# An encoder layer with a seven-product MLP: another order of the up blocks and of the preparation of their inputs, and all weight sums finished in device memory ahead of the MLP

## The chip, the cores and the metric

The kernel runs on one core of one Trainium2 chip. The metric is the device time of one execution in microseconds; a time below is the median of several executions, and the profile shows a single one of them.

## The reference, cut to what matters

One encoder layer (512 tokens, width 1024) and a final norm, all in float32: a token mixer of two kinds of recurrent heads with one input and one output projection, a cross attention over 256 memory tokens, and an MLP of width 4096.

```python
x = x + token_mixer(rmsnorm(x, norm_mix), w_in, b_in, ..., w_out)
x = x + cross_attention(rmsnorm(x, norm_xattn), rmsnorm(mem, norm_mem), w_q, w_kv, w_o)
x = x + squared_relu_mlp(rmsnorm(x, norm_mlp), w_up, w_down)
return rmsnorm(x, norm_final)

def squared_relu_mlp(xn, w_up, w_down):
    return jnp.square(jax.nn.relu(xn @ w_up)) @ w_down
```

## The kernel before

**Products.** Each float32 operand is split in two parts by `split_out` (the line L325): a copy on ACT (ScalarE) gives the high part, a subtraction on DVE (VectorE) the low one, and a product is three matmuls on PE (TensorE): high by high, high by low, low by high. The weights' parts are the tiles `wh` and `wl`. They are held in pools of three buffers, so that the split of a block's weights can begin only when the block three places ahead of it is through on PE. The weights are loaded into tiles `st`, also three buffers, by DMA on SP's queue (L245 before the MLP; L282, L1215 in it).

**The MLP.** It is cut into four quarters, each an up stage (even numbers, 0 to 6) and a down stage (odd, 1 to 7). Every stage is a 2 by 2 block product done with seven products P1 to P7 in place of eight, and each product has two groups a and b, so that a stage has 14 blocks. A block of an up stage is 24 matmuls of 256 columns (the loop over L1559, L1560, L1561), a block of a down stage 12 of 512 columns (L1283, L1284, L1285). The seven products need sums of weights and sums of inputs. The inputs' sums and their splits are the **forms**: for the first up stage they are made in `norm_half` from the normed residual (`times_r` multiplies by the norm's factor, then `part_split` or `split_out`); for a down stage they are made from the squared up results by `first` (L1527, a P5 input), `second` (L1531, P6), `by_p7` (L1539) and `by_p3` (L1535), each an operation on DVE followed by a split. The split's tiles are named `a4` in the program's order and `a` in the profile; `xT` and `yT` are the up stages' inputs, `vv` the residual, `rg` the norm's factor row among others.

**PE's order** is the order in which the code is written; for the MLP that is the table `MORDER`, a string such as "1a 2a 1b" per up stage. DVE, ACT, POOL (GpSimd) and SP each run in the order that a scheduler found from priorities (`tc.high_priority()` moves an operation to the front) and from explicit pairs, `behind(a, b)`. Each engine takes its instructions strictly in that order, so one that waits holds up all behind it. Up results lie in PSUM banks; P1, P5 and P6 are copied out of them on ACT (P5's copy is L1575, P6's L1579), and a product that accumulates in the same bank (P3 on that of P5) waits for the copy.

**The sums of weights.** Some of the weight sums are added by POOL's accumulating DMAs into SBUF tiles `as` while the kernel runs. The others are written once to device memory, as `form_...`, and loaded by L1215 when they are needed. `make_forms` has 80 steps for them: each sum is a copy on SP's queue (L282 from the weights, or L298 from another sum, for a second sum that builds on a first) and an accumulating DMA on POOL (L282). A step is taken on each call of `weights()` from the seventh on, and what is then left over at one step per block of the odd MLP stages, in `mahead`:

```python
        if i >= 6:
            next_form()
        return hl_tiles[i]
```

**Ahead of the MLP** stands the attention's output product; its columns are added to the residual in `add_out` (L1371), the sum of squares goes through POOL (L1420), and small matmuls (L1397, L1438 and their like) turn the row of norm factors into the layout of the inputs. `last_made`, `q_made` and `x_made` hold the instructions of a split, for `behind`.

Of the kernel before, what the change touches and what calls it, by code (L numbers as in the profile page):

```python
# [14 lines left out]
ALU = mybir.AluOpType  # L15
# [65 lines left out]
def trunk(ctx: ExitStack, tc: tile.TileContext, x, mem, wpk, vec, cst, lmask, rmask, rows, out):  # L81
# [177 lines left out]
    def weights(key):  # L259
        i = SIDX[key]  # L260
        with (tc.high_priority() if i > 2 else ExitStack()):
            for n in range(i, i + 3):
                split(n)
            load(i + 3)
        if i >= 6:
            next_form()
        return hl_tiles[i]

# [55 lines left out]
    def split_out(dst_hi, dst_lo, src):  # L324
        return sc.activation(dst_hi, src, AF.Copy), v.tensor_tensor(out=dst_lo, in0=src, in1=dst_hi.bitcast(F32), op=ALU.subtract)  # L325
# [167 lines left out]
    for t, ps in enumerate(acc_v):  # L493
        part_v(t, 3)
        d = VV()
# [700 lines left out]
    seq = lambda s: [("P" + w[0], "ab".index(w[1])) for w in s.split()]  # L1196
    MORDER = []
    for q in range(4):
        MORDER += [seq("1a 2a 1b 6a 5a 7a 3a 4a 5b 6b 2b 7b 3b 4b" if q else "1a 2a 1b 2b 5a 5b 3a 6a 6b 7a 7b 4a 3b 4b"),
                   two(*("P1", "P5", "P6", "P2", "P7", "P3", "P4") if q < 3 else ("P1", "P5", "P2", "P6", "P3", "P7", "P4"))]  # L1200
    MJ = [(st, p, g) for st in range(8) for p, g in MORDER[st]]
    mst, mhl, msum = {}, {}, []
# [29 lines left out]
    def msplit(n):  # L1232
        if n >= len(MJ):
            return
        if n not in mhl:
            for w in [w for w in due if w[0] <= n]:
                due.remove(w)
                w[1](*w[2:])
            st, p, g = MJ[n]
            mload(n)  # L1240
            hi, lo = T("wh", 1024, 3, F32R), T("wl", 1024, 3, F32R)
            last_made[0] = split_out(hi, lo, mst[n])[1]
            mhl[n] = (hi, lo)
            if st % 2 and p == "P6":
                due.append((n + 1, sum_add, st, "P4", g))
            if st % 2 and p in ("P5", "P4") and st < 7:
                q = {"P5": "P5", "P4": "P6"}[p]
                due.append((n + 3, sum_base, st + 2, q, g))
                due.append((n + 7, sum_add, st + 2, q, g))
        return mhl[n]  # L1250
# [117 lines left out]

    def add_out(t, c, ps, sign, last):
        z = xr[t, c]  # L1370
        v.tensor_tensor(out=z, in0=z, in1=ps, op=ALU.add if sign > 0 else ALU.subtract)  # L1371
        if not last:
            return
        with (tc.high_priority() if (t, c) in ((1, 1), (3, 0)) else ExitStack()):
            stats(st2, t, c)
            if (t, c) in ((1, 1), (3, 0)):
                rstd_half(t // 2)
        if (t, c) == (2, 0):
            turn_x2[0] = [smb(), smb()]
            later.append([1, lambda: flip(turn_x2[0], (2,), 0)])  # L1380
        elif (t, c) == (3, 0):
            later.append([0, lambda: flip(turn_x2[0], (3,), 0)])
            later.append([1, lambda: norm_half(1)])
        elif t % 2:
            later.append([0 if (t, c) == (1, 1) else 3, lambda: flip([smb(), smb()], (t - 1, t), c)])
            if (t, c) == (1, 1):
                later.append([1, lambda: norm_half(0)])
# [24 lines left out]
    def rstd_half(u):  # L1412
# [6 lines left out]
        rt[u] = tiny(2)  # L1419
        pool_add[0] = gp.tensor_tensor(out=rt[u], in0=m2_, in1=nh.to_broadcast([P, 2]), op=ALU.pow)  # L1420

    def times_r(x, u, h):
        z = x[:, h * 512:h * 512 + 512]
        r = rrow[:, u * 256:u * 256 + 256]
        v.tensor_tensor(out=z.rearrange("p (k t) -> p k t", t=256), in0=z.rearrange("p (k t) -> p k t", t=256),
                        in1=r.unsqueeze(1).to_broadcast([P, 2, 256]), op=ALU.mult)

    def part_split(p, x, h):
        z = slice(h * 512, h * 512 + 512)
        split_out(xf[p][0][:, z], xf[p][1][:, z], x[:, z])  # L1430

    def norm_half(u):

        ps = smb()
        for t in range(2):
            pe.transpose(ps[:, t * P:t * P + P], rt[u][:, t:t + 1].to_broadcast([P, P]), ident)
        with tc.high_priority():
            sc.activation(rrow[:, u * 256:u * 256 + 256], ps[:, 0:256], AF.Copy)  # L1438
            for p, x in ((("P1", fx[0, 0]), ("P2", fx[0, 1])) if u == 0 else (("P5", sraw[0]),)):
                for h in range(2):  # L1440
                    times_r(x, u, h)
                    part_split(p, x, h)
        if u == 0:
            return
        d = sraw[0]
        x1, x3_, x2_, x4 = fx[0, 0], fx[0, 1], fx[1, 0], fx[1, 1]
        v.tensor_tensor(out=d, in0=d, in1=x1, op=ALU.subtract)
        v.tensor_tensor(out=x3_, in0=x3_, in1=d, op=ALU.add)
        split_out(*xf["P3"], x3_)
        split_out(*xf["P6"], d)  # L1450
        for h in range(2):
            times_r(x2_, 1, h)
        v.tensor_tensor(out=x1, in0=x1, in1=x2_, op=ALU.subtract)
        split_out(*xf["P7"], x1)
        for h in range(2):
            times_r(x4, 1, h)
        split_out(*xf["P4"], x4)

    for p in range(4):
        sta_o[p]["P1"] = tuple(t[:, 0:256] for t in os_[p])  # L1460
# [5 lines left out]
        xf[p] = [YT1()[:, :], YT1()[:, :]]  # L1466
    rrow = RG()
    by_blocks(-1, sta_o, (mm2, mm2, sm2, sm2), add_out, heads_in, after_product)
    msum.append(A16())
    due.extend((2 + g, sum_add, 1, "P5", g) for g in range(2))  # L1470
    due.extend((3 + 2 * g, sum_base, 1, "P6", g) for g in range(2))
# [40 lines left out]
    def up(st):  # L1512
# [8 lines left out]
        def form(p, g, src, buf):  # L1521
            t = buf(F32R)
            split_out(t[:, 0:512], t[:, 512:1024], src)
            forms[p, g] = t

        def first(g):
            v.tensor_tensor(out=y[3, g], in0=y[2, g], in1=y[3, g], op=ALU.subtract)  # L1527
            form("P5", g, y[3, g], A4)
# [11 lines left out]
            form("P7", g, y[0, g], A4)  # L1540

        yt = lambda dt: YT1(dt)
        for n, (p, g) in enumerate(MORDER[st]):
            hi, lo = mahead(len(JOBS) * st + n)
            if p == "P1":
                A[g] = smb()
            if p == "P2":
                B[g] = mmb()
            if p == "P5":
                C[g] = mmb()  # L1550
            ps = B[g] if p == "P2" else C[g] if p in ("P5", "P3") else A[g]
            xh, xl = xf[p]
            for k in range(2):
                o = ps[:, k * 256:k * 256 + 256]
                for kt in range(4):
                    z = slice(k * 512 + kt * P, k * 512 + kt * P + P)
                    m = slice(kt * 256, kt * 256 + 256)
                    new = k == kt == 0 and p in ("P1", "P2", "P5")
                    pe.matmul(o, lhsT=hi[:, z], rhs=xh[:, m], start=new, stop=False, **fl)  # L1559
                    pe.matmul(o, lhsT=hi[:, z], rhs=xl[:, m], start=False, stop=False, **fl)  # L1560
                    pe.matmul(o, lhsT=lo[:, z], rhs=xh[:, m], start=False, stop=kt == 3, **fl)  # L1561
                after_product()
            if p == "P1":
                y[0, g] = msum[g][:, 2048:2560]
                with tc.high_priority():
                    sc.activation(y[0, g], ps, AF.Copy)
            elif p == "P2":
                with tc.high_priority():
                    v.tensor_tensor(out=y[0, g], in0=y[0, g], in1=ps, op=ALU.add)
                square(y[0, g], y[0, g])  # L1570
                form("P1", g, y[0, g], yt)
            elif p == "P5":
                y[3, g] = T2()[:, 0:512]
                with tc.high_priority():
                    sc.activation(y[3, g], ps, AF.Copy)  # L1575
            elif p == "P6":
                y[1, g] = rrow[:, (1 - g) * 512:(1 - g) * 512 + 512]
                with tc.high_priority():
                    sc.activation(y[1, g], ps, AF.Copy)  # L1579
            if p in ("P3", "P6") and {("P3", g), ("P6", g)} <= set(MORDER[st][:n + 1]):  # L1580
                z = y[1, g]
                v.tensor_tensor(out=z, in0=C[g], in1=z, op=ALU.subtract)
                square(z, z)
                form("P2", g, z, G4)
            if p == "P7":
                with tc.high_priority():
                    v.tensor_tensor(out=y[3, g], in0=y[3, g], in1=ps, op=ALU.subtract)
                square(y[3, g], y[3, g])
                form("P4", g, y[3, g], A4)
            elif p == "P4":  # L1590
                y[2, g] = T2()[:, 0:512]
                square(y[2, g], ps)
                first(g)
                if g == 0:
                    second(g)
                    by_p7(g)
                    by_p3(g)
        sta = [{} for _ in range(4)]

        def hand(g):  # L1600
# [114 lines left out]
```

## Time and profile before

| What | Value |
| --- | --- |
| Median of three runs (lowest, highest) | 850.69 us (849.35, 851.29) |
| Profiled execution | 848.46 us |
| Its span | 846.6 us |
| PE, busy | 812.1 us, 96% |
| DVE, ACT, POOL, busy | 620.3, 488.1, 92.4 us |
| DMA moved | 165.16 MB, of it 39.85 MB by POOL's queue |
| MLP's first and last matmul | 492.97 us, 838.04 us |

The profiled execution stands 2.2 us below the median; 1.9 us of it lie outside the span. All times inside the profile count from the span's start. "PE mm L1559 <- ACT t L1575" reads: the matmul of line 1559 into a tile mm waited for ACT's instruction of line 1575, which writes t. A row "690.10:693.50 3.40, 1.66 (x14)" of the table by stretches gives a stretch, its length, and the busy time and number of instructions of each engine in it, then PE's granted clock as a share of full speed and the DMA engines' busy share.

### The profile page before, as it was taken

The page shows a single profiled execution, that of the slowest core. Times are in us where ns is not written, and L with a number is a line of the kernel's source. Part 1 is how long each engine was busy: PE and PEld are TensorE (multiplying, and loading weights), DVE is VectorE, ACT ScalarE, POOL GpSimd, SP SyncE. Part 2 cuts the span into 40 slices and gives each one's busy share as a digit, 9 for nine tenths or more (in the row PEclk, how much of TensorE's full clock was granted, in tenths as well). Part 3 has the DMA queues.
Part 4 walks back from the last instruction along what each step waited for, and adds up shares of the span by engine and source line. Part 5 has one row for each costly group of instructions (what it writes and reads, how often), then busy time and mean ns, then how long its engine had stood idle before and what let it go on. Part 6 is the DMA issues. An engine that isn't in the chain of part 4 may idle for free.

```text
span 846.6 us, 14075 instructions
## 1 busy us (share of the span) xinstructions
PE 812.1 (96%) x5438; PEld 699.7 (83%) x5438; DVE 620.3 (73%) x1033; ACT 488.1 (58%) x854; POOL 92.4 (11%) x132
## 2 busy tenths in 40 slices
PE   8999999999999999999999989989998999999995
PEld 6788788877889988888888879868996799889984
DVE  6568875898479897545669889886487658875885
ACT  5247464536586575445455677833683458446854
POOL 2002000220111201202200011020102000100001
PEclk9999999999999999999999999989999999999998
DMA  7367744494478697877635559589998785768462
GB/s 270 115 232 185 218 146 138 100 223 136 165 176 210 187 301 245 229 220 175 173 102 130 120 134 299 164 213 313 298 304 187 212 263 175 199 202 236 160 149 100
DMA packets 56021, 165.16 MB, mean 195 GB/s; under 512 B 5329, under 2 KB 5457, under 8 KB 55954
## 3 DMA queue, kind: packets, MB, share of 16 engines
q1 hardware_dynamic: 40624, 123.94, 42.1%
q0 software_dynamic: 15040, 39.85, 26.0%
q8 instruction: 43, 0.70, 0.3%
q10 hardware_dynamic: 290, 0.47, 0.2%
q14 instruction: 24, 0.20, 0.1%
HBM read 162.14 MB, written 44.04 MB: 244 GB/s over the span
## 4 chain that ended last, share of the span: by engine, by line
PE 61%; DMA 12%; DVE 11%; issue 7%; ACT 6%; POOL 1%; POOLq 0%; ACTq 0%; SPq 0%; DVEq 0%
PE mm L328 10%; PE mm L330 10%; PE mm L329 9%; DMA st<-form_P 5%; DVE wl L325 5%; PE sm L1283 4%; PE sm L1284 4%; PE sm L1285 4%; DMA st<-in_wpk 4%; ACT wh L325 3%; PE mm L1559 1%; PE mm L1560 1%; PE mm L1561 1%; PE sm L1559 1%; PE sm L1561 1%
## 5 line engine op out<-in xcount | busy, mean ns | idle before, releaser
L325 DVE TENSOR_TENSOR wl<-st,wh 128x1024 fp32r<-128x1024 f32 x163 | 199.0, 1222 | 116.6 <-ACT wh L325 115.2
L325 ACT ACTIVATE wh<-st 128x1024 fp32r<-128x1024 f32 x163 | 172.1, 1058 | 186.5 <-PE mm L329 44.0
L328 PE MATMUL mm<-xT,wh 128*128 128x512 f32 x288 | 115.5, 402 | 0.0
L330 PE MATMUL mm<-xT,wl 128*128 128x512 f32 x288 | 113.2, 393 | 0.1
L329 PE MATMUL mm<-xT,wh 128*128 128x512 f32 x288 | 112.7, 391 | 0.3 <-DVE xT L1042 0.3
L1283 PE MATMUL sm<-wh,a 128*128 128x512 f32 x180 | 71.8, 399 | 7.9 <-ACT a L325 5.9
L1284 PE MATMUL sm<-wl,a 128*128 128x512 f32 x180 | 71.5, 397 | 2.3 <-DVE wl L325 2.3
L1285 PE MATMUL sm<-wh,a 128*128 128x512 f32 x180 | 71.3, 396 | 0.5 <-DVE a L325 0.5
L330 PEld LDWEIGHTS mm<-xT,wl 128*128 128x128 f32 x288 | 54.1, 188 | 11.7 <-DVE wl L325 0.3
L329 PEld LDWEIGHTS mm<-xT,wh 128*128 128x128 f32 x288 | 54.2, 188 | 10.9 <-DVE xT L1042 0.9
L328 PEld LDWEIGHTS mm<-xT,wh 128*128 128x128 f32 x288 | 54.1, 188 | 10.8 <-ACT wh L325 0.3
L282 POOL DMA_DIRECT2D as<-in_wpk x24 | 22.0, 957 | 246.9 <-DVE wl L325 138.8
L282 POOL DMA_DIRECT2D form_P<-in_wpk x40 | 43.4, 1459 | 49.4 <-DMA form_P<-form_P 47.4
L1283 PEld LDWEIGHTS sm<-wh,a 128*128 128x128 f32 x180 | 34.5, 192 | 16.4 <-ACT a L325 6.3
L1284 PEld LDWEIGHTS sm<-wl,a 128*128 128x128 f32 x180 | 34.6, 192 | 10.4 <-DVE wl L325 3.2
L1285 PEld LDWEIGHTS sm<-wh,a 128*128 128x128 f32 x180 | 34.4, 191 | 8.3 <-DVE a L325 1.1
L1560 PE MATMUL sm<-xT,wh 128*128 128x256 f32 x128 | 37.1, 290 | 1.3 <-DVE xT L325 1.2
L1559 PE MATMUL sm<-xT,wh 128*128 128x256 f32 x128 | 37.4, 292 | 0.4 <-ACT xT L325 0.4
L1561 PE MATMUL sm<-xT,wl 128*128 128x256 f32 x128 | 36.9, 288 | 0.0
L325 ACT ACTIVATE wh<-as 128x1024 fp32r<-128x1024 f32 x26 | 27.2, 1054 | 16.7 <-PE sm L1285 9.4
L1559 PE MATMUL sm<-yT,wh 128*128 128x256 f32 x128 | 36.3, 284 | 0.4 <-ACT rg L1579 0.4
L1559 PE MATMUL mm<-xT,wh 128*128 128x256 f32 x128 | 36.6, 286 | 0.0
(388 smaller groups left out, 2129.3 us busy)
## 6 DMA issues: line engine op xcount, KB each, us to landing
st<-in_wpk SPq DMA_DIRECT2D x123, 512.0 KB, 4.6
form_P<-in_wpk POOLq DMA_DIRECT2D x40, 512.0 KB, 10.0
st<-form_P SPq DMA_DIRECT2D x40, 512.0 KB, 5.9
as<-in_wpk POOLq DMA_DIRECT2D x28, 512.0 KB, 8.3
form_P<-in_wpk SPq DMA_DIRECT2D x24, 512.0 KB, 6.7
form_P<-form_P SPq DMA_DIRECT2D x16, 512.0 KB, 6.6
gate<-in_wpk POOLq DMA_DIRECT2D x8, 512.0 KB, 5.5
as<-in_wpk SPq DMA_DIRECT2D x8, 512.0 KB, 4.2
```

Of the source, the lines that this page charges most:

```text
L282: return eng.dma_start(out=dst, in_=mblock(st, g, *b), max_dma_last_dim=4096, **kw)
L325: return sc.activation(dst_hi, src, AF.Copy), v.tensor_tensor(out=dst_lo, in0=src, in1=dst_hi.bitcast(F32), op=ALU.subtract)
L328: pe.matmul(ps, lhsT=ah, rhs=bh, start=first, stop=False)
L329: pe.matmul(ps, lhsT=ah, rhs=bl, start=False, stop=False)
L330: pe.matmul(ps, lhsT=al, rhs=bh, start=False, stop=last)
L1283: pe.matmul(ps, lhsT=ah, rhs=bh, start=new, stop=False, **fl)
L1284: pe.matmul(ps, lhsT=ah, rhs=bl, start=False, stop=False, **fl)
L1285: pe.matmul(ps, lhsT=al, rhs=bh, start=False, stop=end and k == 1, **fl)
L1559: pe.matmul(o, lhsT=hi[:, z], rhs=xh[:, m], start=new, stop=False, **fl)
L1560: pe.matmul(o, lhsT=hi[:, z], rhs=xl[:, m], start=False, stop=False, **fl)
L1561: pe.matmul(o, lhsT=lo[:, z], rhs=xh[:, m], start=False, stop=kt == 3, **fl)
```

## The change

1. `weights()` takes a second step of `make_forms` whenever its number divides by four, so that the steps come to an end ahead of the MLP.
2. `MORDER` has other strings for the up stages. The down stages' strings are as before.
3. In `add_out` the additions for (2,0) and (3,0) get high priority. In `norm_half`, P2's first `times_r` comes behind the second split of P1, and the sum for P3 and its split are moved to the end; the split of the MLP's second block of weights comes behind P1's second split.
4. In the up stages `first` gets high priority, and `by_p3(0)` is called once both of its inputs are there, P4a's result and the P2 form of group a (which needs P3a and P6a): with the new strings that is at P4a in three of the four stages, and at P3a in the first.

The lines behind each edit shift: L1371 becomes L1375, L1425 L1431, L1527 L1539, L1531 L1543, L1535 L1547, L1539 L1551, L1559 to L1561 become L1572 to L1574, L1575 L1588, L1582 L1595, L1283 to L1285 become L1286 to L1288, L1490 L1502.

```diff
-        if i >= 6:
+        for _ in range((i >= 6) + (i >= 6 and i % 4 == 0)):
             next_form()
...
-        MORDER += [seq("1a 2a 1b 6a 5a 7a 3a 4a 5b 6b 2b 7b 3b 4b" if q else "1a 2a 1b 2b 5a 5b 3a 6a 6b 7a 7b 4a 3b 4b"),
+        MORDER += [seq("1a 5a 1b 6a 2a 3a 7a 5b 6b 4a 2b 7b 3b 4b" if q else "1a 1b 2a 2b 5a 5b 6a 6b 7a 7b 4a 3a 4b 3b"),
...
-            last_made[0] = split_out(hi, lo, mst[n])[1]
+            made = split_out(hi, lo, mst[n])
+            last_made[0] = made[1]
+            if n == 1:
+                q_made[0] = made
...
-        v.tensor_tensor(out=z, in0=z, in1=ps, op=ALU.add if sign > 0 else ALU.subtract)
+        with (tc.high_priority() if (t, c) in ((2, 0), (3, 0)) else ExitStack()):
+            v.tensor_tensor(out=z, in0=z, in1=ps, op=ALU.add if sign > 0 else ALU.subtract)
...
-                    times_r(x, u, h)
-                    part_split(p, x, h)
+                    t_ = times_r(x, u, h)
+                    if p == "P2" and h == 0:
+                        behind(t_, x_made[0][1])
+                    made = part_split(p, x, h)
+                    if p == "P1" and h == 1:
+                        x_made[0] = made
...
         v.tensor_tensor(out=d, in0=d, in1=x1, op=ALU.subtract)
-        v.tensor_tensor(out=x3_, in0=x3_, in1=d, op=ALU.add)
-        split_out(*xf["P3"], x3_)
         split_out(*xf["P6"], d)
...
         split_out(*xf["P4"], x4)
+        v.tensor_tensor(out=x3_, in0=x3_, in1=d, op=ALU.add)
+        split_out(*xf["P3"], x3_)
...
+    for a, b in zip(q_made[0], x_made[0]):
+        behind(a, b)
...
+                done.add(("P2", g))
+                if ("P4", 0) in done and g == 0:
+                    by_p3(0)
...
-                first(g)
+                with tc.high_priority():
+                    first(g)
+                done.add(("P4", g))
                 if g == 0:
                     second(g)
                     by_p7(g)
-                    by_p3(g)
+                    if ("P2", 0) in done:
+                        by_p3(g)
```

Where the written order and the scheduler move instructions shows in the rows of each engine's order. `a4_`, `xT_`, `t2_` and the like are tiles with their number, `wl<-st,wh` is a weight split.

First place, DVE in stage 1 (the first down stage), before: `t2_823` is the tile that `first` and `second` of group b rework, `a4_854` the low part of P5b's input, `a4_863` that of P6b's; `wl_867` and `wl_870` are the weights of P6a and P6b.

```order
L325 TENSOR_TENSOR wl_867_5691<-as_792_5111,wh_866_5690 128x1024
L325 TENSOR_TENSOR a4_846_5567<-as_739_4829,a4_846_5567 128x512
L325 TENSOR_TENSOR a4_847_5571<-rg_700_4641,a4_847_5571 128x512
L325 TENSOR_TENSOR wl_870_5711<-as_792_5111,wh_869_5710 128x1024
L1527 TENSOR_TENSOR t2_823_5356<-t2_853_5636,t2_823_5356 128x512
L325 TENSOR_TENSOR a4_854_5640<-t2_823_5356,a4_854_5640 128x512
L1531 TENSOR_TENSOR t2_823_5356<-t2_823_5356,as_792_5111 128x512
```

The same place after; P5b's input is now `a4_851`, made from the L1539 row.

```order
L1539 TENSOR_TENSOR t2_823_5372<-t2_850_5618,t2_823_5372 128x512
L325 TENSOR_TENSOR a4_843_5549<-as_739_4845,a4_843_5549 128x512
L325 TENSOR_TENSOR wl_858_5662<-as_739_4845,wh_857_5661 128x1024
L1547 TENSOR_TENSOR rg_700_4657<-rg_700_4657,t2_818_5338 128x512
L1595 TENSOR_TENSOR rg_700_4657<-mm_822_5347,rg_700_4657 128x512
L1502 TENSOR_TENSOR vv_528_3640<-vv_528_3640,sm_855_5659 128x512
L325 TENSOR_TENSOR wl_861_5680<-as_739_4845,wh_860_5679 128x1024
L1502 TENSOR_TENSOR vv_529_3642<-vv_529_3642,sm_856_5660 128x512
L325 TENSOR_TENSOR a4_851_5622<-t2_823_5372,a4_851_5622 128x512
```

`first` of group b and the split of P5b's input moved from behind the weights of P6a and P6b to ahead of both.

A little later on DVE, after: the rows of `second` of group b (L1543) and of P6b's input `a4_863`; `wl_874` and `wl_877` are the weights of P2a and P2b.

```order
L325 TENSOR_TENSOR wl_874_5753<-st_859_5665,wh_873_5752 128x1024
L1543 TENSOR_TENSOR t2_823_5372<-t2_823_5372,as_792_5127 128x512
L1551 TENSOR_TENSOR as_792_5127<-as_792_5127,t2_850_5618 128x512
L1547 TENSOR_TENSOR rg_700_4657<-rg_700_4657,t2_823_5372 128x512
L325 TENSOR_TENSOR wl_877_5771<-st_862_5683,wh_876_5770 128x1024
L325 TENSOR_TENSOR a4_863_5701<-t2_823_5372,a4_863_5701 128x512
```

`second` stood one row behind the split of P5b's input before; now seven rows, three of them weight splits, lie between, and P6b's split stands behind P2b's weights.

Second place, DVE at the start of the first up stage, before: `xT_692` is the tile of the inputs of P1 (from `a4_752`) and P2 (from `a4_783`), each split in two halves; `wl_779` and `wl_794` are the weights of the second and third block.

```order
L325 TENSOR_TENSOR xT_692_4631<-a4_752_4913,xT_692_4631 128x512
L325 TENSOR_TENSOR wl_779_5033<-st_758_4941,wh_778_5032 128x1024
L325 TENSOR_TENSOR wl_794_5114<-st_763_4967,wh_793_5113 128x1024
L325 TENSOR_TENSOR xT_692_4631<-a4_752_4913,xT_692_4631 128x512
L325 TENSOR_TENSOR xT_692_4631<-a4_783_5054,xT_692_4631 128x512
L1425 TENSOR_TENSOR a4_783_5054<-a4_783_5054,rg_700_4641 128x512
L1371 TENSOR_TENSOR vv_531_3634<-vv_531_3634,mm_702_4643 128x512
```

After, from the same first row on; `wl_801` and `wl_805` are the weights of the fourth and fifth block, `a4_798` is P5's input, L1421 and L1422 are two steps towards the second half's norm factors.

```order
L325 TENSOR_TENSOR xT_692_4647<-a4_752_4929,xT_692_4647 128x512
L325 TENSOR_TENSOR wl_779_5049<-st_758_4957,wh_778_5048 128x1024
L1421 TENSOR_TENSOR tiny_789_5121<-misc_75 128x2
L325 TENSOR_TENSOR wl_794_5130<-st_763_4983,wh_793_5129 128x1024
L1422 TENSOR_SCALAR tiny_790_5122<-tiny_789_5121 128x2
L1414 TENSOR_TENSOR a4_798_5157<-a4_797_5152,a4_770_5028 128x512 x2
L1431 TENSOR_TENSOR a4_783_5070<-a4_783_5070,rg_700_4657 128x512
L325 TENSOR_TENSOR wl_801_5201<-st_766_5001,wh_800_5200 128x1024
L1431 TENSOR_TENSOR a4_798_5157<-a4_798_5157,rg_700_4657 128x512 x2
L325 TENSOR_TENSOR xT_692_4647<-a4_783_5070,xT_692_4647 128x512
L325 TENSOR_TENSOR wl_805_5233<-st_777_5046,wh_804_5232 128x1024
L325 TENSOR_TENSOR xT_693_4648<-a4_798_5157,xT_693_4648 128x512 x2
```

P1's second half moved ahead of the weights of the second block, and P2's second half, which is the row behind these, stands behind the weights of the fifth block and both halves of P5's input.

Third place, POOL's queue from the MLP's first down stage on, before; the rows named `form_` are accumulating DMAs of `make_forms`, those named `as_` the sums added on chip.

```order
L282 DMA as_739_4829<-in_wpk 128x1024 x2
L282 DMA form_4_P6_0_3329<-in_wpk 256x1x512
L282 DMA form_6_P6_0_3341<-in_wpk 256x1x512
L282 DMA form_4_P6_1_3333<-in_wpk 256x1x512
L282 DMA as_792_5111<-in_wpk 128x1024 x2
L282 DMA form_6_P6_1_3345<-in_wpk 256x1x512
L282 DMA form_4_P4_0_3330<-in_wpk 256x1x512
L282 DMA form_6_P4_0_3342<-in_wpk 256x1x512
L282 DMA as_792_5111<-in_wpk 128x1024
L282 DMA form_4_P4_1_3334<-in_wpk 256x1x512
L282 DMA as_792_5111<-in_wpk 128x1024
L282 DMA form_6_P4_1_3346<-in_wpk 256x1x512
```

After, with the rows of the norm's factors (L1424) that stand ahead of the MLP, and ahead of them the last of the sums that are made before the MLP:

```order
L282 DMA form_4_P4_0_2899<-in_wpk 256x1x512
L282 DMA form_6_P4_0_2911<-in_wpk 256x1x512
L282 DMA form_4_P4_1_2903<-in_wpk 256x1x512
L1163 DMA gate_630_4302<-in_wpk 128x1024
L1163 DMA gate_631_4303<-in_wpk 128x1024
L1163 DMA gate_630_4302<-in_wpk 128x1024
L1163 DMA gate_631_4303<-in_wpk 128x1024
L1424 TENSOR_TENSOR tiny_774_5040<-tiny_773_5037,misc_75 128x2
L1424 TENSOR_TENSOR tiny_791_5125<-tiny_790_5122,misc_75 128x2
L282 DMA as_739_4845<-in_wpk 128x1024 x2
L282 DMA as_792_5127<-in_wpk 128x1024 x2
L282 DMA form_6_P4_1_2915<-in_wpk 256x1x512
```

All of them but one moved ahead of the MLP, and so did the second sums' copies on SP's queue (L298).

More of the change, by code (lines that the diff above doesn't have):

```diff
@@ L1420, in rstd_half @@
         pool_add[0] = gp.tensor_tensor(out=rt[u], in0=m2_, in1=nh.to_broadcast([P, 2]), op=ALU.pow)
+    x_made = [None]
     def times_r(x, u, h):
@@ L1424, in times_r @@
         r = rrow[:, u * 256:u * 256 + 256]
-        v.tensor_tensor(out=z.rearrange("p (k t) -> p k t", t=256), in0=z.rearrange("p (k t) -> p k t", t=256),
+        return v.tensor_tensor(out=z.rearrange("p (k t) -> p k t", t=256), in0=z.rearrange("p (k t) -> p k t", t=256),
                         in1=r.unsqueeze(1).to_broadcast([P, 2, 256]), op=ALU.mult)
@@ L1429, in part_split @@
         z = slice(h * 512, h * 512 + 512)
-        split_out(xf[p][0][:, z], xf[p][1][:, z], x[:, z])
+        return split_out(xf[p][0][:, z], xf[p][1][:, z], x[:, z])
     def norm_half(u):
@@ L1542, in up @@
         yt = lambda dt: YT1(dt)
+        done = set()
         for n, (p, g) in enumerate(MORDER[st]):
```

## The prediction

> **What bounds the kernel now.** I read the shares of busy time first, then the table by stretches with the MLP's eight stages as stretches, then what PE waited for.
>
> ```profile
> PE 812.1 (96%) x5438; PEld 699.7 (83%) x5438; DVE 620.3 (73%) x1033; ACT 488.1 (58%) x854; POOL 92.4 (11%) x132
> ```
>
> PE is busy for 96% of 846.6 us. The change removes no matmul, so all it can win is PE's idle time and the clock lost behind it. The stretches are stages 0 to 7 (even ones up, odd ones down) and the tail.
>
> ```profile
> 492.97:539.84 46.87, 43.81 (x345) 42.81 (x344) 40.80 (x50) 34.75 (x54) 5.27 (x6) 0.96 0.80 225
> 539.84:585.48 45.64, 39.72 (x171) 32.41 (x170) 35.68 (x46) 22.54 (x28) 6.65 (x7) 0.93 0.83 227
> 585.48:627.63 42.15, 40.60 (x337) 40.40 (x336) 28.30 (x33) 28.27 (x40) 4.93 (x5) 1.00 1.01 303
> 627.63:672.78 45.15, 41.28 (x170) 32.37 (x169) 30.92 (x39) 20.65 (x25) 5.78 (x6) 0.96 0.83 218
> 672.78:716.58 43.80, 42.06 (x338) 41.85 (x337) 30.44 (x35) 31.05 (x44) 1.73 (x2) 0.96 0.71 219
> 716.58:754.68 38.10, 38.10 (x170) 31.53 (x169) 29.05 (x36) 18.56 (x21) 3.49 (x4) 1.00 0.70 194
> 754.68:798.57 43.89, 42.07 (x338) 41.86 (x336) 30.34 (x35) 31.05 (x44) 1.73 (x2) 0.96 0.71 216
> 798.57:838.04 39.47, 38.55 (x170) 31.28 (x168) 31.90 (x46) 22.27 (x35) 2.84 (x4) 1.00 0.44 121
> 838.04:846.60 8.56, 0.00 (x0) 0.00 (x0) 2.44 (x5) 2.17 (x4) 1.54 (x2) 0.63 0.32 123
> ```
>
> The second number is the length, the third PE's busy time. Stage 5 has no idle time and the full clock: 38.1 us is what a down stage takes undisturbed, 12 matmuls of a block in 2.72 us (38.10/168 = 0.227 each). Stage 2 without its idle time is 40.6 us, the same for an up stage: 0.121 each, 2.9 us a block. Against these floors the eight stages stand 6.3, 7.5, 1.6, 7.1, 3.2, 0, 3.3 and 1.4 us too high, 30 us together. PE's waits over the MLP, in us, times and longest:
>
> ```profile
> PE sm L1283 <- ACT a L325: 5.9, 1, 5.9
> PE mm L1559 <- ACT t L1575: 5.1, 3, 1.8
> PE sm L1284 <- DVE wl L325: 2.3, 3, 0.8
> PE sm L1560 <- DVE xT L325: 1.2, 1, 1.2
> PE sm L1283 <- ACT wh L325: 1.1, 1, 1.1
> PE sm L1397 <- DVE vv L1371: 0.9, 1, 0.9
> PE sm L1283 <- DVE vv L1490: 0.9, 1, 0.9
> PE sm L1285 <- DVE a L325: 0.5, 1, 0.5
> PE sm L1559 <- ACT xT L325: 0.4, 1, 0.4
> ```
>
> They make 18.3 us. The rest is the granted clock and the pipe that refills behind a gap. Three stretches of 3.4 us show the clock:
>
> ```profile
> 690.10:693.50 3.40, 1.66 (x14) 1.54 (x14) 1.82 (x2) 2.16 (x3) 0.00 (x0) 1.00 0.74 269
> 693.50:696.90 3.40, 3.40 (x19) 3.40 (x18) 2.31 (x3) 3.07 (x5) 0.00 (x0) 0.50 0.62 195
> 607.80:611.20 3.40, 3.40 (x31) 3.40 (x30) 2.78 (x4) 2.93 (x5) 0.00 (x0) 1.00 1.03 287
> ```
>
> A stretch with 1.74 us idle is followed by one at half clock, in which 19 matmuls start where 31 do undisturbed: 12 x 0.11 = 1.3 us for each such stretch. The Trainium skill, "TensorE: Matmul & The Clock Gate", section "HAM oscillation — how this bites in real kernels", gives the rule that PE must have no idle gap over about 3.4 us; the trace disagrees, since here 1.74 us was enough, and the measurement decides. By the page's rule the two stalls that I expect below, of 2.7 and 3.4 us, would cost no clock, and my sum would be 2.6 us lower.
>
> **The change, part by part.** *The forms' priority, stage 1.* The 5.9 us is P5b, the fourth block:
>
> ```profile
> 552.71 0.68 DVE L1527 TENSOR_TENSOR t<-t,t 128x512 f32<-128x512 f32 x1
> 553.43 0.63 ACT L325 ACTIVATE a<-t 128x512 fp32r<-128x512 f32 x1 [4.09 <-DVE t L1527]
> 554.09 0.69 DVE L325 TENSOR_TENSOR a<-t,a 128x512 fp32r<-128x512 f32 x1 [0.69 <-ACT a L325]
> ...
> 553.50:556.90 3.40, 2.79 (x7) 2.17 (x8) 2.75 (x5) 1.82 (x4) 1.35 (x2) 0.50 1.04 200
> ```
>
> ACT had nothing to do for 4.09 us: `first` of group b stood in DVE's queue behind the weights of P6a and P6b, and the latter wait for a buffer. In the new order it stands ahead of both. The last weights ahead of its split are now P5b's, which take the buffer of P1a, free 2.7 us into the stage: 2.72 + 1.06 + 1.22 (splits, from the rows below) + 0.68 + 0.69 (an addition and its own split) = 6.4 us, where PE wants it after three blocks, at 8.2. So 5.92 goes, and the half clock behind it: the row of 553.5 has clock 0.50 and 2.8 us of work, 1.4 us of it the clock's: 45.6 - 7.3 = 38.3. But `second` and P6b's split now stand behind P2a's and P2b's weights. The latter reuse the buffer that P6a frees, so P6b's low part comes after P6a's end by a weight split on ACT, one on DVE and its own:
>
> ```profile
> L325 DVE TENSOR_TENSOR wl<-st,wh 128x1024 fp32r<-128x1024 f32 x163 | 199.0, 1222 | 116.6 <-ACT wh L325 115.2
> L325 ACT ACTIVATE wh<-st 128x1024 fp32r<-128x1024 f32 x163 | 172.1, 1058 | 186.5 <-PE mm L329 44.0
> ```
>
> 1.06 + 1.22 + 0.69 = 3.0 us, while P6b starts at P6a's end and does two matmuls without it (0.45): a stall of some 2.6 us, with refill 2.7, and 1.3 of clock. Ends: 0 (another row frees it) and 4.5. Stage 1: 38.3 + 4.0 = 42.3, that is -3.3.
>
> *The start, stage 0.* The waits on xT (0.4 and 1.2) and on L1371 (0.9) come from DVE doing two weight splits ahead of P1's second half and the residual's last addition. All three now stand ahead of one or both: -2.6. L1422, a step of the second norm row, now stands behind one of the splits (1.22), so I leave 1.0 of waiting there. Late next is P2a, now the third block: its second half stands behind the fifth block's weights, which wait for P1b's end, where P2a begins. From there 1.06 + 1.22 + 3 x 0.6 = 4.1 us until the half is there; PE has six matmuls of 0.12 for that time, so it waits 3.4, and the half clock that followed the first gaps (1.3) now follows this one. Stage 0: -2.6 + 1.0 + 3.4 = +1.8; since the other small matmuls of the norm fall into full clock, I take +1.5. Ends: -3 (no wait at P2a) and +3.
>
> *The up order.* L1559 waits for L1575 three times, once in each of stages 2, 4 and 6: P3a accumulates in P5a's bank and only P7a lies between, while the copy of P5a is behind a weight split on ACT. In the new order four blocks (11.6 us) lie between in these stages, and the other products that follow in a bank have two blocks between, or stand as before, where no wait shows. Stages 2, 4, 6: to their floor plus 0.2, 40.8 each: -1.4, -3.0, -3.1. P3's input, moved to the end in stage 0, is covered by the 11 blocks ahead of P3a. Ends: all 7.5, or half.
>
> *The sums, stage 3.* Its five waits are for weights and what they hold up (2.3 + 1.1 + 0.5), and the chain shows why:
>
> ```profile
> 648.68 13.51 DMA st<-in_wpk
> ```
>
> A load took 13.5 us to land. In the same stretch lie the last of these:
>
> ```profile
> L282 POOL DMA_DIRECT2D form_P<-in_wpk x9: 1030/1052/1438, 516.8 to 641.3; - x9
> L298 SPq DMA_DIRECT2D form_P<-form_P x8: 475/476/487, 564.0 to 623.8; - x8
> ```
>
> Nine accumulating DMAs and eight copies ran between 516.8 and 641.3; eight and eight of them now run ahead of the MLP, and the DMA share of stages 0 to 3 (0.80, 0.83, 1.01, 0.83) should come down to that of 4 and 5 (0.71, 0.70). Stage 5, the same stage without sums, has no idle time. Stage 3: 38.5, that is -6.6; ends 38.1 and 43 (the waits stay, their clock goes).
>
> *The same sums, ahead of the MLP.* Two rows of the page give the price:
>
> ```profile
> q1 hardware_dynamic: 40624, 123.94, 42.1%
> q0 software_dynamic: 15040, 39.85, 26.0%
> ```
>
> POOL's 39.85 MB are 76 DMAs of 0.52 MB; 26.0% of 846.6 us over 76 is 2.9 us of all 16 engines each. SP's 123.94 MB in 42.1% make 1.5 us per 0.52 MB. Eight of each: 35 us of DMA time, moved into these stretches:
>
> ```profile
> 170.00:200.00 30.00, 29.66 (x428) 22.88 (x427) 30.00 (x53) 12.84 (x21) 4.93 (x7) 1.00 0.85 207
> 200.00:290.00 90.00, 88.74 (x588) 78.58 (x586) 67.61 (x150) 59.11 (x136) 11.76 (x21) 1.00 0.62 176
> 290.00:385.00 95.00, 93.53 (x499) 78.45 (x500) 65.02 (x145) 54.56 (x141) 12.74 (x14) 1.00 0.81 236
> 385.00:492.97 107.97, 107.70 (x549) 90.60 (x548) 76.56 (x141) 61.54 (x124) 13.70 (x16) 1.00 0.58 139
> ```
>
> Free there: 0.15 x 30 + 0.38 x 90 + 0.19 x 95 + 0.42 x 108 = 102 us, and PE is busy for 319.6 of the 323 us. On SP and POOL the steps stand ahead of weight loads and of additions on chip; a step issues in 0.5 us on SP and 1.0 to 1.4 on POOL, and weights are loaded three blocks early. So 0, with ends 0 and +6. The cover is the free time between 385 and 493: were it gone, loads would land as in stage 3.
>
> *Stages 5 and 7* may wait as stage 1 does for P5b: +0.4 and +0.1. The tail stays.
>
> Sum: +1.5 - 3.3 - 1.4 - 6.6 - 3.0 + 0.4 - 3.1 + 0.1 = -15.4. The profiled execution, 848.46, becomes 833.1; it stood 2.2 below the median of 850.69, which becomes 835.2.
>
> **The rivals.** *Both new stalls fail to come*, because PE reaches P2a and P6b later than I add up: for it speaks that every sum of rows here is by hand; against it, that both stand in the queue behind splits whose buffer is freed at the very start of the block in need. -8.7: 826.5.
>
> *Stage 3's lateness isn't the sums'.* Loads in it are also held by DVE's splits and by the additions on chip, which stay. Against: stage 5 has those too. It would keep 45.15: 841.8.
>
> *Slower.* The sums pile up where the DMA engines are full: between 170 and 200 and 290 and 385 only 4.5 + 18 = 22.5 us are free. If all 35 us fell there, weights would come 12.5 us late; with the half clock behind each gap (1.3 for 1.74 idle, a factor of 1.7) PE loses 21 us, against 15.4 won: 856. It decides from 9 us of lateness on. For it: PE's only weights there come by the same engines, and a 13.5-us landing was seen at a share of 0.83. Against: steps are spread over 40 calls. The Trainium skill, "DMA: Bandwidth & Descriptors", section "Issuing engines are not separate DMA queues", speaks for it: DMAs of SP, ACT and GpSimd run on the same 16 engines and interleave, so POOL's sums do not pass beside SP's loads. The late landing in stage 3 agrees.
>
> *Nothing to see*: gains and new stalls of like size, from 849 to 852.4.
>
> **Chances.** The forecast 0.68 (on its own 829 to 840, its stalls at either end), both stalls absent 0.12, stage 3 as before 0.12, slower 0.05, nothing 0.03. What a measurement can tell from no change is 0.2%, 1.7 us. Faster: 0.68 + 0.12 + 0.12 = 0.92; same 0.03; slower 0.05. For 8 in 10 the range takes in most of the forecast's own, half of the first rival and the second: 828 to 842.
>
> **What would show it.** No wait of L1572 for L1588; a wait at P2a (L1573 for xT) near 502 and one at P6b (L1288 or L1286 for a) in stage 1, each before a stretch at half clock; stage 3 near 38.5 us with a DMA share near 0.70, no form DMA but one behind 493; the first MLP matmul near 493. I am wrong if that matmul comes several us later, or if stages 0 and 1 have other waits than these.

## The result, and the profile after

The changed kernel's median over five executions is 843.1 us (841.41 to 845.0), the kernel before took 849.35 us beside it (848.9 to 851.29): ratio 0.9921, 95% interval 0.99 to 0.9942. It is faster by 6.3 us, where 15.5 were forecast, and lies above the range that was given. The profiled execution is the slowest of the five, 845.0 us with a span of 843.2, so its stages add up to 3.4 us won, not 6.3. One execution in the experiments, E1's profiled one, was slow (899.07 us at a granted clock of 0.844) and is left out of E1's ratio and of every comparison of stages.

The table by stretches of the changed kernel, stages 0 to 7 of the MLP and the tail (start and end, length, busy time of PE, its weight loads, DVE, ACT and POOL, then PE's granted clock, the DMA share and GB/s):

```profile
495.06:548.94 53.88, 47.14 (x346) 46.33 (x344) 41.80 (x52) 36.42 (x54) 7.98 (x6) 0.87 0.70 199
548.94:594.33 45.39, 41.53 (x170) 33.19 (x169) 34.08 (x44) 21.35 (x27) 3.52 (x4) 0.92 0.63 170
594.33:635.35 41.02, 40.92 (x338) 40.47 (x337) 27.21 (x30) 28.07 (x39) 1.73 (x2) 1.00 0.72 224
635.35:674.15 38.80, 38.55 (x171) 31.38 (x170) 32.12 (x42) 20.49 (x25) 3.49 (x4) 1.00 0.69 197
674.15:714.46 40.31, 40.31 (x338) 40.31 (x336) 27.04 (x30) 28.06 (x39) 1.73 (x2) 1.00 0.74 227
714.46:753.46 39.00, 38.55 (x171) 31.39 (x169) 32.19 (x42) 20.55 (x25) 3.49 (x4) 1.00 0.70 198
753.46:794.25 40.79, 40.55 (x338) 40.37 (x337) 26.45 (x30) 28.07 (x39) 1.73 (x2) 1.00 0.70 221
794.25:834.51 40.26, 38.96 (x170) 31.12 (x168) 35.69 (x52) 24.49 (x39) 2.85 (x4) 1.00 0.45 130
834.51:843.20 8.69, 0.00 (x0) 0.00 (x0) 2.44 (x5) 2.17 (x4) 1.54 (x2) 0.78 0.32 121
```

Stages 2, 3, 4 and 6 came down to within 0.7 us of the floors (40.3 for an up stage, as in stage 4, and 38.1 for a down stage), with the full clock. Stage 0 grew by 7.0 us at a mean clock of 0.87, stage 1 stayed, and the MLP begins 2.1 us later. PE's waits in the MLP (total, times, longest) name three culprits, and the waits ahead of the MLP two that were smaller or absent before:

```profile
PE sm L1288 <- DVE a L325: 3.7, 5, 1.7
PE mm L1573 <- DVE xT L325: 3.2, 1, 3.2
PE sm L1442 <- POOL tiny L1424: 3.2, 1, 3.2
PE sm L1286 <- ACT a L325: 1.8, 1, 1.8
...
PE sm L860 <- ACT as L854: 1.4, 1, 1.4
PE sm L553 <- DVE t L540: 1.3, 1, 1.3
```

The wait on L1573 is the forecast one at P2a, the waits on a (1.8 and 1.7) are the forecast one at P6b. The one on POOL was not forecast at this size. POOL's power for the second norm factors works on 128x2 elements; both executions of that line, after and before (duration least, median, most in ns):

```profile
L1424 POOL TENSOR_TENSOR tiny<-tiny,misc x2: 711/2056/3402, 490.2 to 499.2; 128x2 f32<-128x2 f32 x2
```

```profile
L1420 POOL TENSOR_TENSOR tiny<-tiny,misc x2: 692/702/712, 488.1 to 499.3; 128x2 f32<-128x2 f32 x2
```

The second one took 3.40 us in place of 0.69. What DVE did meanwhile, from the timeline of the changed kernel:

```profile
498.93 0.16 DVE L1422 TENSOR_SCALAR tiny<-tiny 128x2 f32<-128x2 f32 x1
499.00 1.28 DVE L1414 TENSOR_TENSOR a<-a,a 128x512 f32<-128x512 f32 x2
500.20 0.69 DVE L1431 TENSOR_TENSOR a<-a,rg 128x512 f32<-128x512 f32 x1
500.80 1.22 DVE L325 TENSOR_TENSOR wl<-st,wh 128x1024 fp32r<-128x1024 f32 x1
503.77 1.29 DVE L1431 TENSOR_TENSOR a<-a,rg 128x512 f32<-128x512 f32 x2 [1.75 <-ACT rg L1444]
```

POOL started at 499.18 and ended at 502.58, 0.56 us after DVE's row of operations with two SBUF inputs stopped (500.80 + 1.22 = 502.02). Before the change DVE happened to pause there: it stood idle from 499.21 us to 499.58, while POOL worked from 499.30 on.

```profile
499.04 0.17 DVE L1418 TENSOR_SCALAR tiny<-tiny 128x2 f32<-128x2 f32 x1
499.58 1.42 DVE L1410 TENSOR_TENSOR a<-a,a 128x512 f32<-128x512 f32 x2 [0.37 <-ACT a L1404]
```

That DVE's row of such operations slows POOL is the theory that the experiments test first.

### The profile page after: what moved, and what is told of

Its sections match the earlier page's. It is cut to its first block, busy times and chain, and to the rows that moved or that the text cites. A ratio compares the mean times of both kernels' runs of the same rounds, so it can differ in the third digit from the quotient of the medians.

```text
span 843.2 us, 14062 instructions
## 1 busy us (share of the span) xinstructions
PE 813.8 (97%) x5438; PEld 700.4 (83%) x5438; DVE 619.5 (73%) x1033; ACT 486.7 (58%) x854; POOL 94.6 (11%) x132
## 3 DMA queue, kind: packets, MB, share of 16 engines
q1 hardware_dynamic: 40624, 123.94, 41.7%
## 4 chain that ended last, share of the span: by engine, by line
PE 64%; DVE 12%; DMA 10%; issue 7%; ACT 5%; POOL 1%; POOLq 0%; ACTq 0%; DVEq 0%
PE mm L328 9%; PE mm L330 9%; PE mm L329 9%; DVE wl L325 4%; PE sm L1288 4%; PE sm L1286 4%; PE sm L1287 4%; DMA st<-in_wpk 3%; ACT wh L325 2%; DMA st<-form_P 2%; PE mm L1573 2%; PE sm L1572 2%; PE mm L1574 2%; PE sm L1574 2%; PE mm L1572 2%
## 5 line engine op out<-in xcount | busy, mean ns | idle before, releaser
L1288 PE MATMUL sm<-wh,a 128*128 128x512 f32 x180 | 71.9, 399 | 3.7 <-DVE a L325 3.7
L1286 PE MATMUL sm<-wh,a 128*128 128x512 f32 x180 | 71.1, 395 | 2.1 <-ACT a L325 1.8
L1288 PEld LDWEIGHTS sm<-wh,a 128*128 128x128 f32 x180 | 34.3, 191 | 13.4 <-DVE a L325 6.4
L1286 PEld LDWEIGHTS sm<-wh,a 128*128 128x128 f32 x180 | 34.2, 190 | 10.0 <-ACT a L325 2.5
L1573 PE MATMUL mm<-xT,wh 128*128 128x256 f32 x128 | 37.6, 294 | 3.2 <-DVE xT L325 3.2
L1572 PE MATMUL sm<-xT,wh 128*128 128x256 f32 x128 | 37.6, 294 | 0.2 <-DVE t L1603 0.2
L1573 PE MATMUL sm<-xT,wh 128*128 128x256 f32 x128 | 37.5, 293 | 0.3 <-DVE xT L325 0.2
L1574 PE MATMUL mm<-xT,wl 128*128 128x256 f32 x128 | 37.5, 293 | 0.1
L1572 PE MATMUL mm<-xT,wh 128*128 128x256 f32 x128 | 37.4, 292 | 0.0
```

What stands on the lines that cost most here:

```text
L1286: pe.matmul(ps, lhsT=ah, rhs=bh, start=new, stop=False, **fl)
L1288: pe.matmul(ps, lhsT=al, rhs=bh, start=False, stop=end and k == 1, **fl)
```

## The experiments

All ratios are to the kernel before, run beside on the same chip, with the 95% interval. Lengths of stages are from the profiled execution of each kernel, by the first matmuls of the stages.

**E1, the sums alone.** The kernel before with edit 1 only:

```diff
-        if i >= 6:
+        for _ in range((i >= 6) + (i >= 6 and i % 4 == 0)):
```

> The kernel before with edit 1 alone: the second step of make_forms whenever the number of the weights divides by four, nothing else. Theory A (the sums made stage 3 late, and moving them costs nothing ahead of the MLP): stage 3 goes from 45.2 to about 38.8 us as in the changed kernel, stage 2 and the rest stay, first MLP matmul at 493; ratio 0.992, some 6.4 us. Rival B (the sums cost the 2 us by which the changed kernel's MLP began later, 495.06 against 492.97): first matmul at 495, ratio 0.995. Rival C (stage 3's lateness came from the order of the up stages): stage 3 stays near 45, ratio 1.00.

Ratio 0.9947 (0.9921 to 0.9972), 4.5 us (0.0053 of 848.75). Rival C is out, since the interval leaves out 1.00. There are no stages to compare for this kernel; between A (0.992) and B (0.995) the value is nearer to B, but the interval reaches to both.

**E2, the up order alone.** The kernel before with the later up stages' strings, `first` under high priority and `by_p3` when its inputs are there:

```diff
-"1a 2a 1b 6a 5a 7a 3a 4a 5b 6b 2b 7b 3b 4b" if q
+"1a 5a 1b 6a 2a 3a 7a 5b 6b 4a 2b 7b 3b 4b" if q
...
-                first(g)
+                with tc.high_priority():
+                    first(g)
```

> The kernel before with the new strings of the up stages 2, 4 and 6, first under high priority and by_p3 as soon as its inputs are there; start and sums as before. Theory A: the waits of P3a for P5a's copy go (1.1, 3.5 and 3.1 us in stages 2, 4 and 6), and stage 1 loses the 5.9 us wait but gets the wait at P6b (the DVE queue is full there), so stage 1 stays near 45; stage 3 stays at 45; ratio 0.990 to 0.992, some 7 us. Rival: the waits of stages 2, 4 and 6 went because the sums were gone from the DMA engines; then they stay here and the ratio is 1.00.

Ratio 0.9936 (0.9914 to 0.9958). Its stages 0 to 4 by stretches:

```profile
493.77:544.67 50.90, 45.33 (x345) 44.32 (x344) 42.94 (x53) 37.00 (x57) 5.27 (x6) 0.93 0.77 217
544.67:586.37 41.70, 38.91 (x170) 31.30 (x169) 33.43 (x43) 20.32 (x25) 6.65 (x7) 1.00 0.86 238
586.37:629.57 43.20, 41.43 (x337) 40.55 (x337) 25.90 (x29) 26.68 (x37) 4.93 (x5) 1.00 0.97 282
629.57:675.17 45.60, 41.23 (x170) 32.28 (x169) 33.35 (x42) 21.89 (x27) 5.78 (x6) 0.96 0.85 230
675.17:715.47 40.30, 40.30 (x338) 40.26 (x337) 26.97 (x30) 28.07 (x39) 1.73 (x2) 1.00 0.73 226
```

Stage 4 is at its floor with the order alone, and stage 3 is as late as before: the two gains are separate, as forecast. P3a's waits for P5a's copy are gone in all three stages. (They were 1.55, 1.74 and 1.82 us long; the 1.1, 3.5 and 3.1 named above are what the stages lost in length.) Stage 2 still takes 43.2 us while the sums fill its DMA share to 0.97, so the order alone doesn't win it. Stage 1 takes 41.7 us here and not the 45 expected of it, though P6b waits as forecast (1.7 and 1.0 us): the clock stays full. Stage 0, whose string is as before, grows from 46.9 to 50.9 us, with a wait of 2.9 us for P6's copy that was 0.4 before. No term of the forecast has this, and its cause was not tried.

**E3, the old start.** The changed kernel with the first stage's string, `add_out`, `norm_half` and the two `behind` as before:

```diff
-"1a 1b 2a 2b 5a 5b 6a 6b 7a 7b 4a 3a 4b 3b"
+"1a 2a 1b 2b 5a 5b 3a 6a 6b 7a 7b 4a 3b 4b"
...
-    for a, b in zip(q_made[0], x_made[0]):
-        behind(a, b)
```

> The changed kernel with the first up stage's string, add_out and norm_half (and the two pairs of behind) as before, all else as changed. Theory A: stage 0 returns from 53.9 to about 47 us, since both its waits (3.2 for L1442, 3.2 for L1573) come from the new order of the start; ratio 0.983 to 0.986. Rival (the waits in stage 0 come from the sums' DMAs or POOL's queue): stage 0 stays near 54 and the ratio at 0.992.

Ratio 0.9865 (0.9837 to 0.9894): the new start costs about 5 us. Stage 0 came to 49.4 us, not 47, with the wait for P6's copy that E2 shows (here 2.1 us). Stage 1 came to 41.8, so it is the new start that made it worse in the changed kernel (45.4). POOL's second power took 0.69 us again. In what the code does, this kernel is E2's with edit 1 added: stage 2 goes from 43.2 to 40.3 us, stage 3 from 45.6 to 38.7.

**E4, DVE stands still for POOL.** The changed kernel with a small copy that reads POOL's result ahead of L1414, on the same engine:

```diff
+                seen = tiny(2)
+                seen_made = v.tensor_copy(out=seen, in_=rt[1])
-                    v.tensor_tensor(out=sraw[0][:, z], ...)
+                    behind(v.tensor_tensor(out=sraw[0][:, z], ...), seen_made)
```

> The changed kernel with one small copy on DVE that reads POOL's result of the second norm factors, ahead of the subtraction of L1414 in flip: DVE stands still while POOL computes, instead of running operations with two SBUF inputs beside it. Theory A (such DVE work holds POOL's access to SBUF): POOL's L1424 goes from 3.40 back to 0.7 to 1.4 us, the wait of the flips' matmul (3.2 us) falls to under 1.2, and with one stretch of half clock less the kernel gains 2 to 4 us over the changed one: ratio 0.987 to 0.990. Rival B (POOL was slow for its own sake, say after 8 us of idleness): L1424 stays at 3.4, DVE waits for it too, and the kernel gets no faster: ratio 0.992 or worse.

Ratio 0.9878 (0.985 to 0.9906); the kernel became faster by making DVE wait. POOL's line, shifted by two:

```profile
L1426 POOL TENSOR_TENSOR tiny<-tiny,misc x2: 712/887/1062, 491.3 to 500.2; 128x2 f32<-128x2 f32 x2
```

1.06 us in place of 3.40: one DVE operation (0.69) still lay beside it. The wait of the flips' matmul fell from 3.2 to 0.9 and stage 0 from 53.9 to 46.8; stage 1 stayed slow (46.5). Theory A holds, B falls.

**E7 and E8, the lock by itself.** E4 with one more addition of 128x1024 on DVE at the moment when POOL gets its input, its second input in SBUF (E7) or in PSUM (E8); the sum is overwritten:

```diff
+                extra = v.tensor_tensor(out=sraw[0], in0=fx[0, 0], in1=..., op=ALU.add)
```

> E4's kernel with one more operation on DVE straight behind L1422 (here L1427), that is at the moment at which POOL gets its input: an addition of 128x1024 with two inputs in SBUF (1.22 us; its result is overwritten later, the output doesn't change). DVE then waits for POOL by the small copy. Theory A (DVE with two SBUF inputs keeps POOL out of SBUF): POOL's operation takes 0.69 plus the rest of the addition, 1.6 to 1.9 us. Rival B (POOL is slow by itself at this place): its time doesn't depend on DVE, 0.7 or 3.4.

> The same as the run with two SBUF inputs, but the second input of the added operation is a PSUM bank; same size, same place. Theory A: POOL isn't kept out, 0.7 us (0.6 to 0.9), though DVE is as busy. A second theory C (any busy DVE slows POOL): 1.6 to 1.9 as with SBUF. Rival B: as before, the same in both.

E7's addition on DVE, and POOL:

```profile
500.33 1.22 DVE L1413 TENSOR_TENSOR a<-a 128x1024 f32<-128x1024 f32 x1
...
500.50 1.60 POOL L1429 TENSOR_TENSOR tiny<-tiny,misc 128x2 f32<-128x2 f32 x1 [8.23 <-DVE tiny L1427]
```

E8's:

```profile
498.82 1.22 DVE L1413 TENSOR_TENSOR a<-a,sm 128x1024 f32<-128x1024 f32 x1
...
499.00 0.69 POOL L1429 TENSOR_TENSOR tiny<-tiny,misc 128x2 f32<-128x2 f32 x1 [8.23 <-DVE tiny L1427]
```

The same work for DVE, at the same place: 1.60 us with two SBUF inputs, 0.69 with one. Each kernel was run once (842.84 and 840.97 us), so there is no ratio; the reading is POOL's row alone. Here it isn't a busy DVE that holds POOL up, but one with two inputs in SBUF (in E7 both are parts of one tile). In the changed kernel, in E4 and in E7 alike POOL ended 0.55 to 0.56 us after the last of these operations. The Trainium skill, "GPSIMD Engine Reference", section "1. Specifications", says that POOL's SBUF interfaces are shared with VectorE and contended by its operations with two SBUF inputs; the runs agree (1.60 against 0.69 us), and add that POOL in the changed kernel waited through four such operations in a row.

**E5, P2 first.** E4 with both halves of P2's split ahead of the fourth and fifth blocks' weights and of P5's preparation (`copied` is ACT's copy of the second half's norm factors):

```diff
+            if n in (3, 4):
+                for m in p2_made:
+                    for a, b in zip(made, m):
+                        behind(a, b)
...
+            if u == 1:
+                [behind(copied, m[0]) for m in p2_made]
...
+                    if p == "P5" and h == 0:
+                        [behind(t_, m[1]) for m in p2_made]
```

> E4's kernel with both halves of P2's split ahead of the weights of the fourth and fifth block and of P5's preparation, on DVE and ACT. Theory A (P2a waits because its second half stands in DVE's queue behind the fifth block's weights, as forecast): the waits of L1573 in stage 0 (3.2 us in the changed kernel, 0.9 and 2.1 in E4) fall to under 0.5, stage 0 from 46.8 to 43 to 44 us; ratio about 0.984. Rival (P2a's inputs are late for the norm row): the wait stays at 2 us or more and stage 0 at 46 to 47. In both, stage 1 stays at 45 to 46 us with its wait at P6b, since DVE is busy without a break there.

Ratio 0.9849 (0.9822 to 0.9877). The waits at P2a are gone, but stage 0 takes 49.4 us, 2.6 more than E4's: PE now waits 2.0 and 1.5 us at P6a, four blocks on. Theory A on the place was right, on the price wrong: the stall moved. What E5 has over E4 lies elsewhere. Stage 1, where nothing was meant to change, takes 42.7 in place of 46.5, against the 45 to 46 expected: DVE's rows there stand in another order too, and the second of P6b's waits is 0.7 us in place of 1.7.

**E6, and P6b first.** E5 with `second` of group b under high priority:

```diff
                 if (p, g) == at:
-                    fn(1)
+                    with (tc.high_priority() if fn is second else ExitStack()):
+                        fn(1)
```

> The run before it (P2 first) with the call of second for group b under high priority, so that P6b's input is split ahead of P6b's, P2a's and P2b's weights. Theory A (the order of DVE's queue makes P6b wait): the waits before P6b (1.8 and 1.7 us) go and with them a stretch of half clock, stage 1 from 45 or 46 to 41 or 42 us; ratio about 0.980. Rival B (DVE's total work in stage 1 is the bound, whatever its order): another block waits as long instead, and stage 1 stays within 1 us.

Ratio 0.981 (0.978 to 0.984), 831.81 us, with stage 0 as in E5 (49.3). Stage 1 of E5 and of E6:

```profile
544.10:586.80 42.70, 40.35 (x170) 32.59 (x170) 32.82 (x43) 20.40 (x24) 3.52 (x4) 0.96 0.61 173
```

```profile
543.70:581.80 38.10, 38.10 (x170) 31.55 (x169) 32.44 (x43) 20.00 (x24) 3.52 (x4) 1.00 0.69 194
```

DVE does the same 32 us of work, PE is busy throughout at the full clock: the order of the queue was the cause, not its load. Rival B falls; the stage came out lower than the 41 to 42 expected.

**E9, P6's input sooner in stage 0.** E6 with the subtraction and split for P6 under high priority:

```diff
+        with tc.high_priority():
             v.tensor_tensor(out=d, in0=d, in1=x1, op=ALU.subtract)
             split_out(*xf["P6"], d)
```

> E6's kernel with the subtraction for P6's input in norm_half and its split under high priority. Theory A (in stage 0 the wait has wandered to P6a, 1.9 and 1.5 us before L1584 and L1585, since its input is made behind the weights of the seventh and eighth block, which come late): both waits go and a stretch of half clock with them, stage 0 from 49.3 to about 44 us; ratio 0.975 to 0.977. Rival (late weights from the DMA are the cause): the wait stays at the block's weights, stage 0 at 48 or more.

Ratio 0.9806 (0.9781 to 0.983), no gain on E6; stage 0 took 47.9 us in place of 49.3, where 44 were expected. The waits of 1.9 and 1.5 at P6a became 0.5 and 0.9 there and 1.4 and 1.2 at P7a, eight us later. The trace speaks for the rival, the late weights: ACT stands idle for 3.7 us before a weight split at 512 and for 3.2 before one at 521, each time for a load; DVE's half of the split stands behind it, and the split of P6a's or P7a's inputs behind that.

```profile
511.96 1.06 ACT L325 ACTIVATE wh<-st 128x1024 fp32r<-128x1024 f32 x1 [3.66 <-DMA st<-form_P]
521.20 1.06 ACT L325 ACTIVATE wh<-st 128x1024 fp32r<-128x1024 f32 x1 [3.18 <-DMA st<-form_P]
```

No run changes these loads alone, so this is read, not shown.

**E10, the second steps elsewhere.** E9 with another spread of the extra steps:

```diff
-        for _ in range((i >= 6) + (i >= 6 and i % 4 == 0)):
+        for _ in range((i >= 6) + (i >= 16 and i % 3 == 0)):
```

> E9's kernel with the second step of make_forms on other calls: when the number divides by three, from the sixteenth on (17 calls in place of 16, none of them at the start). Theory A (the sums cost time ahead of the MLP where the DMA engines are full: seven adding DMAs in a row at 73 us, and 1.3 us of PE waiting at 83 us in each kernel with the sums ahead): the wait at 83 us goes, the MLP begins 1.3 us or more earlier, at about 493; ratio 0.0015 lower than E9's. Rival (that wait has another cause): it stays, and the ratio is E9's.

831.01 us, ratio 0.9787 (0.9766 to 0.9807), the best here; the intervals of E9 and E10 overlap, so the gain between them isn't shown by the times. The trace shows the wait: PE in the stretch of 80 to 100 us, in E9 and then in E10:

```profile
80.00:100.00 20.00, 18.68 (x306) 14.58 (x307) 18.14 (x28) 10.24 (x15) 0.77 (x1) 1.00 1.07 262
```

```profile
80.00:100.00 20.00, 20.00 (x329) 15.77 (x329) 17.98 (x29) 10.34 (x15) 0.00 (x0) 1.00 1.08 277
```

The 1.3 us are gone, so the early extra steps caused them. The DMA share is the same and full in both, so it doesn't tell how. The order of the queues does show a way: in E9 one more copy of a sum and a weight load stand on SP's queue ahead of a small load (L750, a mask for two scans of the token mixer), which is issued at 60.58 us in place of 54.74. On DVE both scans that read the mask (L768) then stand behind a weight split and start at 67.93, where the first of them starts at 62.99 in E10, and the row that PE waits for (L540) comes at 82.62 in place of 81.30. This is read from the traces, not tested by itself. Of the 1.3 us 0.9 reaches the MLP, which begins at 493.76 in place of 494.69. The wait on L854 at 308 us is 1.5 here and 1.0 in E9; it goes from 0.4 to 2.2 over the kernels, and no run shows what sets it.

## Why the prediction was right and wrong, point by point

- *Stage 3, the sums:* forecast -6.6, measured 45.15 to 38.80, -6.4, with the DMA share down from 0.83 to 0.69. E2 and E3, which differ by edit 1, show that it is theirs. Right.
- *The up order:* forecast -1.4, -3.0, -3.1 in stages 2, 4 and 6; measured -1.1, -3.5, -3.1. Right; E2 adds that stage 2 needed the sums gone too.
- *Stage 0, the step that failed most:* forecast +1.5, measured +7.0. The stall at P2a was right in place and size (3.4 against 3.2). For the second norm row I left 1.0 us, on the count of L1422 behind one weight split; it cost 3.2, since I took POOL's power at its 0.7 us, and the operations with two SBUF inputs that DVE now runs beside it held it to 3.40 (E4, E7 and E8). The clock was under-priced too: I took one stretch at half clock, 1.3 us, for all gaps of the start. A gap of 3.2 us cost more than the one of 1.74 from which I had the price, here after the wait on POOL:

```profile
500.80:504.20 3.40, 1.57 (x8) 1.57 (x9) 1.65 (x3) 0.96 (x3) 3.40 (x3) 0.60 0.75 242
504.20:507.60 3.40, 3.40 (x18) 3.40 (x17) 1.47 (x3) 0.06 (x1) 0.13 (x1) 0.50 0.83 227
```

  The work right after the gap is slow already (8 matmuls in 1.57 us, where 13 fit at 0.121), and so is the next stretch (18 for 28): 0.6 + 1.2, about 1.8 us. Behind the stall at P2a it is 9 matmuls in 1.91 us and then 18 again, about 2.0. Of the 5.5 us by which the term was off, 2.2 are the wait on POOL and some 2.5 the clock; I can't place the rest, about 1 us.
- *Stage 1:* forecast -3.3, measured -0.2. That the 5.9 us at P5b goes was right (0.4 is left), and so was the place of the new stall. Its size, 2.7, was not: 1.8 + 1.7 were measured, and a longer slow clock. The 1.8 are for the high part from ACT, which I took as ready at P6b's start; it waits for `second`. I counted only the buffer that P6a frees; but DVE had next to no pause from the stage's start on:

```profile
548.90:568.80 19.90, 16.04 (x67) 12.33 (x66) 19.83 (x27) 12.90 (x19) 2.66 (x3) 0.94 0.61 136
```

  so `second` came when everything ahead of it in the queue was done. E6 shows it: with `second` moved forward both waits go. The size of the loss is the clock's in good part: E3, with waits of 1.7 and 1.0 us at the same place, keeps the clock at 1.00 and takes 41.8 us; the changed kernel has 0.92 and 45.4.
- *Ahead of the MLP:* forecast 0 with an end of +6, measured +2.1: waits of 1.3 at 83 us and 1.4 in place of 0.4 at 309 us. I weighed only free DMA time from 170 us on; E10 shows that the extra steps ahead of 83 us made the first wait. What lengthened the second stays open.
- *Stages 5 and 7:* forecast +0.5 together, measured +0.9 and +0.8.
- *The sum:* -15.4 forecast, -3.4 in this execution and -6.3 in the median. Of the 12.0 us that this execution lacks, 5.5 lie in stage 0, 3.1 in stage 1, 2.1 ahead of the MLP and 1.2 in stages 5 and 7. The forecast's own sign of being wrong came true: stage 0 has a wait that it did not name. The rival with both stalls absent (826.5) did not happen by itself; E6, which takes away the stall at P6b and moves that at P2a, reached 831.8.

## What to carry to other kernels

When an edit reorders a queue, work out when each operation comes from the sum of the work ahead of it as well as from the buffers it waits for, and look at what now runs beside a small operation of another engine on a chain that PE waits for. A stall that is taken away is worth its length only if the next operation in line is ready; here P2a's moved to P6a and P6a's in part to P7a. What a pause of PE cost here was its length plus the slow clock behind it, where there was one, and one price per pause did not fit.

## What the runs showed of the hardware

- A POOL operation of 0.69 us took 3.40 us beside four DVE operations with two SBUF inputs, 1.60 beside one, and 0.69 beside one with an input in PSUM. Letting DVE wait 0.6 us came with a kernel some 4 us faster (ratios 0.9921 and 0.9878, whose intervals just overlap), and with a stage 0 of 46.8 us in place of 53.9.
- The clock that a pause costs did not follow from its length alone. In stage 1, waits of 1.7 and 1.0 us at P6b left the mean clock at 1.00 (E2, E3), 1.7 and 0.7 went with 0.96 (E5), and 1.8 and 1.7 with 0.92 (the changed kernel). What decides it was not tried.
- Executions of one kernel differ by nearly 1% on one chip: eighteen of the kernel before, in one series, took 844.7 to 852.41 us, at mean granted clocks of 0.981 to 0.993. That the stretches at half clock fall differently each time would fit, but was not tried.
